# Channel MLP: the second product by seven half-size block products, token-major output

## Chip, cores and metric

One core of one Trainium2 chip. The metric is device time in microseconds (us), median of the runs of one program; lower is better. The program is written in Python for the five engines of the core: TensorE (PE, matmuls), VectorE (DVE), ScalarE (ACT), GpSimd (POOL) and SyncE (SP, here only a DMA queue).

## What is computed

A one-layer trunk over 512 tokens of 1,024 channels. Two gated branches and an output projection end in the residual `x`; then comes the part that the change touches:

```
h2 = RMSNorm(x) * g_ffn
f  = square(relu(h2 @ W_up))          # 512 x 4096
x  = x + f @ W_down                   # 4096 -> 1024
out = RMSNorm(x) * g_final            # 512 x 1024
```

All is float32. Each operand of a product is split exactly into two parts (`hi`, `lo`) of the type fp32r, and a product is three matmuls: hi·hi, hi·lo, lo·hi.

## The kernel before, in words

Channels lie on the 128 partitions and tokens on the free axis (`T` = 512), so a tile is 128x512. Weights come as a stream of units of eight 128x128 blocks (512 KB), in the order of use, each into a buffer `wraw`. `split` (L87) writes `whi` on ACT (a copy that rounds) and `wlo` on DVE (raw minus hi, both read from SBUF). `blocks` (L136) hands out the blocks; at each new unit it issues the splits of this unit and the next two, and the loads of the three behind them. `wraw`, `whi` and `wlo` have three buffers each, so a split can run two units ahead of the matmuls and no further. A column tile (`col_tile`, L154) takes one unit in most stages: 24 matmuls of 512 columns into one PSUM bank, with the weight block as the stationary operand and the activations moving.

The order on each engine is made when the program is built: a list scheduler takes, for each engine, the ready instruction that stands first in the program. `later(n, fn)` and `tick()` put work off by column tiles.

The MLP works in four chunks of 1,024 hidden channels. `up(c)` (L512) makes eight column tiles; per tile DVE takes relu times the row scale out of PSUM (L508), ACT squares it (L509), and `parts` splits it into `f_jh`, `f_jl`. Then come eight column tiles `dn` over the chunk (L526), each added to the residual tile `x2[j]` by DVE (L527). In the last chunk four tiles (`dl`) are done whole, and four (`dh`) by halves of the tokens, with 256 columns per matmul (L595 to L602), so that the final norm of one half can run beside the matmuls of the other. The final norm (`post` L539, `rms_out` L554, `finish` L569) sums squares over the partitions by matmuls with ones, spreads 1/rms by a product with a diagonal, and scales the residual tiles. The output is channel-major and is transposed on the host.

GpSimd does little: sums of squares (L191, L493) and one product per recurrent tile (L421). One pool, `tp`, holds 78 tiles of 128x512 for everything but the weights.

Of the kernel before, what the change touches and what calls it, by code (L numbers as in the profile page):

```python
# [30 lines left out]
# order of the column tiles between the spatial gating's inputs and the output projection  # L31
# [18 lines left out]

@with_exitstack
def trunk(ctx: ExitStack, tc: tile.TileContext, xT, wall, lruw, wsT, par, ln, out):
# [5 lines left out]
    tp = ctx.enter_context(tc.tile_pool(name="tp", bufs=78))  # L58
    ps = ctx.enter_context(tc.tile_pool(name="ps", bufs=8, space=bass.MemoryType.PSUM))

    def t2(name, dt=F32, shape=None):
        return tp.tile(shape or [P, T], dt, tag="t2", name=name)

    def psum(name):
        return ps.tile([P, T], F32, tag="ps", name=name)

# [36 lines left out]
    now = [0]  # L103
    due = {}

# [9 lines left out]
    raws, units = {}, {}  # L115
    n_stream = n_units - KT // 2
    pos = [0]

    def load_unit(u, pieces=1):
        if u < n_stream and u not in raws:  # L120
            raws[u] = wp.tile([P, UB * P], F32, tag="wraw", name=f"wraw{u}")
            n = UB * P // pieces
            for i in range(pieces):
                nc.sync.dma_start(out=raws[u][:, i * n : (i + 1) * n], in_=wall[u][:, i * n : (i + 1) * n])

    def split_unit(u, pieces=1):
        if u < n_stream and u not in units:
            hi = wp.tile([P, UB * P], F32R, tag="whi", name=f"whi{u}")
            lo = wp.tile([P, UB * P], F32R, tag="wlo", name=f"wlo{u}")
            n = UB * P // pieces  # L130
            for i in range(pieces):
                sl = slice(i * n, (i + 1) * n)
                split(raws[u][:, sl], hi[:, sl], lo[:, sl])
            units[u] = (hi, lo)

    def blocks(n=1):  # L136
        u, s = divmod(pos[0], UB)
        if s == 0:
            units.pop(u - 1, None)
            split_unit(u)  # L140
            split_unit(u + 1)
            split_unit(u + 2)
            for i in range(3, 6):
                load_unit(u + i)
        pos[0] += n
        sl = slice(s * P, (s + n) * P)
        return units[u][0][:, sl], units[u][1][:, sl]
# [34 lines left out]
    def x_in(k):  # L182
        xg[k] = parts(f"xg{k}", xts[k], pc(C_GMIX + k))
# [61 lines left out]
    u_t = [[t2(f"u{b}_{h}") for h in range(2)] for b in range(NB)]  # L245
# [46 lines left out]
    # softplus(-lam) = max(-lam, 0) + log1p(exp(-|lam|)), log1p(e) = 2 atanh(e / (2 + e))  # L292
# [26 lines left out]
    # layer norm of v, one group of channels  # L319
# [15 lines left out]
    # mixing over positions, gating by u, back to channels on partitions  # L335
# [56 lines left out]
        # per head, its channels' both parts stacked along the contraction  # L392
# [11 lines left out]
    def lru_gates(j, xr, xs):  # L404
# [12 lines left out]
        # 1 - a^2 = tanh(-log a) (1 + a^2)  # L417
# [61 lines left out]
    x2, x2g = [], []  # L479
    ssq2 = t2("ssq2")  # L480
    for j in range(KT):
        xt = t2(f"xres{j}")
# [3 lines left out]
        x2g.append(parts(f"x2{j}", xt, pc(C_GFFN + j)))  # L486
# [19 lines left out]
    def up_out(f, name, acc):  # L506
        t = t2(name)
        nc.vector.scalar_tensor_tensor(out=t, in0=acc, scalar=0.0, in1=r2_b, op0=ALU.max, op1=ALU.mult)  # L508
        nc.scalar.activation(t, t, AF.Square)  # L509
        f.append(parts(name, t))  # L510

    def up(c):  # L512
        f = []
        for j in range(FT):
            acc = col_tile(f"up{c}_{j}", x2g)
            if c == 0:
                later(1, lambda acc=acc, j=j: up_out(f, f"f{c}_{j}", acc))
# [13 lines left out]
    f = up(NCH - 1)  # L531
    HT = T // 2
    HK = KT // 2
    HB = NB // 2
    r3 = const.tile([P, NB], F32, name="r3")

    ssq3 = t2("ssq3")

    def post(j, acc, b0, b1):  # L539
        sl = slice(b0 * P, b1 * P)  # L540
        nc.vector.tensor_tensor(out=x2[j][:, sl], in0=acc, in1=x2[j][:, sl], op=ALU.add)  # L541
        if j == 0:
            nc.scalar.activation(ssq3, x2[j], AF.Square)
            return
        sq = t2(f"sqc{j}_{b0}")
        nc.scalar.activation(sq[:, sl], x2[j][:, sl], AF.Square)  # L546
        if j < KT - 1:
            nc.vector.tensor_tensor(out=ssq3[:, sl], in0=ssq3[:, sl], in1=sq[:, sl], op=ALU.add)
        return sq

    # 1/rms with tokens on partitions, then spread over the partitions by a product with its diagonal
    dg = {}

    def rms_out(h):  # L554
        b0, b1 = h * HB, (h + 1) * HB
        ms3 = [psum(f"ms3_{b}") for b in range(b0, b1)]
        for i, s in enumerate((ssq3, sq7[h])):
            for b in range(b0, b1):
                nc.tensor.matmul(
                    ms3[b - b0][:, 0:2], s[:, b * P : (b + 1) * P], ones[:, 0:2], start=i == 0, stop=i == 1  # L560
                )
# [33 lines left out]
    for h in range(2):  # L595
        sl = slice(h * HT, (h + 1) * HT)
        for j in range(HK, KT):
# [5 lines left out]
            if h == 1 and j == HK:  # L603
                rms_out(0)
# [78 lines left out]
```

## Time and profile before

| what | us |
|---|---|
| median of 3 runs (lowest, highest) | 815.52 (815.16, 816.07) |
| span of the profiled execution, first to last instruction | 814.2 |
| PE busy, share of the span | 804.2, 99% |
| DVE busy | 450.9, 55% |
| ACT busy | 398.2, 49% |
| POOL busy | 39.8, 5% |

No time beside its span is listed for the profiled execution; the median lies 1.3 us above the span, which is what lies around it. "Busy" is the time in which an engine has an instruction under way. A line such as "L90 DVE TENSOR_TENSOR wlo<-wraw,whi 128x1024" names the line of the kernel, the engine, the operation, what it writes and reads, and its shape; a number in brackets at the end is the idle time before it and what ended it.

### The profile page before, as it was taken

The numbers are of one execution on the slowest core, as the hardware profiler recorded it, in microseconds if no ns is written. First come the engines' busy times: TensorE is split into PE (matmuls) and PEld (weight loads), VectorE is DVE, ScalarE is ACT, GpSimd is POOL, SyncE is SP. The second block draws the span as 40 slices with busy tenths as digits, with TensorE's granted clock in tenths as the row PEclk, the third lists the DMA queues.
The fourth block names the chain that finished last, engine by engine and source line by source line (L and its number), as shares of the span: only waits on it lengthen the run. The fifth ranks groups of instructions, "written<-read, shape, count | busy, mean of one in ns | idle before, by whom it ended". The sixth has DMA issues, their size and how long they took to land.

```text
span 814.2 us, 9244 instructions
## 1 busy us (share of the span) xinstructions
PE 804.2 (99%) x3656; PEld 669.8 (82%) x3656; DVE 450.9 (55%) x627; ACT 398.2 (49%) x505; POOL 39.8 (5%) x44
## 2 busy tenths in 40 slices
PE   9999999999999999999999999999999999999995
PEld 8788888888888888888888888888888888888895
DVE  5868775786566566665544554344333443344435
ACT  6453546868788888852234443124322432233411
POOL 4200000000000000000003100000000000000000
PEclk9999999999999999999999999999999999999997
DMA  7523321223323233333244322322332233223202
GB/s 261 175 98 117 116 91 56 101 69 103 114 77 107 88 104 103 104 104 103 84 137 155 103 92 93 114 88 94 103 104 85 97 104 104 83 98 121 87 1 103
DMA packets 27595, 84.27 MB, mean 103 GB/s; under 512 B 3233, under 2 KB 5281, under 8 KB 27553
## 3 DMA queue, kind: packets, MB, share of 16 engines
q1 hardware_dynamic: 23728, 77.67, 28.6%
q10 hardware_dynamic: 3824, 6.03, 2.4%
q8 instruction: 28, 0.46, 0.2%
q14 instruction: 15, 0.11, 0.0%
HBM read 81.59 MB, written 2.10 MB: 103 GB/s over the span
## 4 chain that ended last, share of the span: by engine, by line
PE 96%; POOL 1%; DMA 1%; SPq 0%; DVE 0%; ACT 0%; issue 0%; DVEq 0%; POOLq 0%
PE up L152 7%; PE up L150 7%; PE up L151 7%; PE dn L152 5%; PE dn L150 5%; PE u L225 5%; PE dn L151 5%; PE v L225 3%; PE g L150 2%; PE x L152 2%; PE x L150 2%; PE g L152 2%; PE ba L152 2%; PE ba L151 2%; PE x L151 2%; PE g L151 2%
## 5 line engine op out<-in xcount | busy, mean ns | idle before, releaser
L89 ACT ACTIVATE whi<-wraw 128x1024 fp32r<-128x1024 f32 (+1 forms) x139 | 145.3, 1051 | 289.8 <-PE dn L151 101.4
L90 DVE TENSOR_TENSOR wlo<-wraw,whi 128x1024 fp32r<-128x1024 f32 (+1 forms) x139 | 170.8, 1229 | 40.0 <-ACT whi L89 39.7
L508 DVE SCALAR_TENSOR_TENSOR f<-up,r_b 128x512 f32<-128x512 f32 x32 | 22.1, 691 | 79.9 <-PE up L152 79.8
L527 DVE TENSOR_TENSOR xres<-dn,xres 128x512 f32<-128x512 f32 x24 | 16.6, 692 | 78.3 <-PE dn L152 78.3
L425 DVE SCALAR_TENSOR_TENSOR w<-w,s 128x512 f32<-128x512 f32 x10 | 6.9, 692 | 59.3 <-ACT w L420 59.3
L389 DVE SCALAR_TENSOR_TENSOR xr<-xrp,par_sb,xr 128x512 f32<-128x512 f32 x30 | 22.5, 750 | 0.7
L395 ACT ACTIVATE xra<-xr 64x512 fp32r<-64x512 f32 x10 | 6.3, 633 | 31.3 <-DVE xr L389 31.3
L421 POOL TENSOR_TENSOR ig<-ig,xr 128x512 f32<-128x512 f32 x10 | 12.9, 1287 | 156.6 <-ACT ig L415 144.8
L509 ACT ACTIVATE f<-f 128x512 f32<-128x512 f32 x32 | 19.8, 619 | 1.4 <-DVE f L508 1.4
L546 ACT ACTIVATE sqc<-xres 128x256 f32<-128x256 f32 (+1 forms) x11 | 5.2, 476 | 29.0 <-DVE xres L541 29.0
L493 POOL TENSOR_TENSOR ssq<-ssq,sqb 128x512 f32<-128x512 f32 x7 | 11.5, 1649 | 100.5 <-issue 79.6
L485 DVE TENSOR_TENSOR xres<-o,xres 128x512 f32<-128x512 f32 x8 | 5.5, 691 | 19.7 <-PE o L152 17.2
L452 ACT ACT_TABLE_LOAD x11 | 14.1, 1283 | 0.2
L415 ACT ACTIVATE ig<-gate,par_sb 64x512 f32<-64x512 f32 x20 | 13.7, 684 | 0.4
L415 ACT ACTIVATE rg<-gate,par_sb 64x512 f32<-64x512 f32 x20 | 13.7, 683 | 0.4
L437 ACT ACT_TABLE_LOAD x10 | 12.8, 1283 | 0.3 <-DVE gr L436 0.2
L426 ACT ACT_TABLE_LOAD x10 | 12.8, 1283 | 0.2
L418 ACT ACT_TABLE_LOAD x10 | 12.8, 1283 | 0.2
L150 PE MATMUL up<-x20h,whi 128*128 128x512 f32 x32 | 12.9, 402 | 0.0
L151 PE MATMUL up<-x27l,whi 128*128 128x512 f32 x32 | 12.5, 390 | 0.0
L150 PE MATMUL up<-x22h,whi 128*128 128x512 f32 x32 | 12.5, 390 | 0.0
L152 PE MATMUL up<-x24h,wlo 128*128 128x512 f32 x32 | 12.5, 390 | 0.0
(953 smaller groups left out, 2372.1 us busy)
## 6 DMA issues: line engine op xcount, KB each, us to landing
wraw<-in_wall SPq DMA_DIRECT2D x137, 512.0 KB, 3.3
xt<-in_xT SPq DMA_DIRECT2D x8, 256.0 KB, 6.2
xres<-in_xT ACTq DMA_DIRECT2D x8, 256.0 KB, 2.6
lr<-in_wall SPq DMA_DIRECT2D x8, 256.0 KB, 5.7
lwr<-in_lruw ACTq DMA_DIRECT2D x5, 256.0 KB, 2.7
ln<-in_ln ACTq DMA_DIRECT2D x4, 256.0 KB, 5.0
out_yT<-o ACTq DMA_DIRECT2D x4, 256.0 KB, 2.3
wraw<-in_wall SPq DMA_DIRECT2D x2, 256.0 KB, 4.1
```

The lines of the kernel that those rows point to most:

```text
L89: nc.scalar.activation(hi, src, AF.Copy)
L90: nc.vector.tensor_tensor(out=lo, in0=src, in1=hi.bitcast(F32), op=ALU.subtract)
L150: nc.tensor.matmul(acc, lhs[0], rhs[0], start=start, stop=False)
L151: nc.tensor.matmul(acc, lhs[0], rhs[1], start=False, stop=False)
L152: nc.tensor.matmul(acc, lhs[1], rhs[0], start=False, stop=stop)
L225: nc.tensor.matmul(acc[b], xg[k][xi][:, b * P : (b + 1) * P], w[wi], start=k == 0 and i == 0, stop=k == KT - 1 and i == 2,)
L389: nc.vector.scalar_tensor_tensor(out=xr, in0=xrp[:, 1 + k : 1 + k + T], scalar=pc(C_CW + k * RT + j), in1=xr, op0=ALU.mult, op1=ALU.add)
L415: nc.scalar.activation(dst[o], acc[n][src], AF.Sigmoid, bias=par_sb[o, c + j : c + j + 1])
L452: nc.scalar.activation(gs, gs, AF.Sigmoid)
L508: nc.vector.scalar_tensor_tensor(out=t, in0=acc, scalar=0.0, in1=r2_b, op0=ALU.max, op1=ALU.mult)
L509: nc.scalar.activation(t, t, AF.Square)
L527: nc.vector.tensor_tensor(out=x2[j], in0=acc, in1=x2[j], op=ALU.add)
```

## The change

Per chunk the second product is a product of A (512 tokens x 1,024 hidden) with B (1,024 hidden x 1,024 channels). Both are cut into 2x2 blocks of 512, and seven products of blocks and of sums of blocks replace the eight (the Winograd form of Strassen's scheme; `PRODUCTS` is their order). Now the activations are the stationary operand and the weights move, so the result has tokens on partitions.

- **Weights**: W_down comes as eight raw tiles of 128x1024 per chunk, loaded during `up(c)`. `sum_item` makes the sums of the weight blocks on GpSimd, in place: two instructions of 128x1024 each for p5, p6, p7, p4. Each of the 14 items (seven products, two halves) is then split like a unit, through the same three buffers.
- **Activations**: `up_out` squares into 128x(4x256) tiles `a11`..`a22`. `factor` makes `s5`, `s6` on DVE and two sums (for p3, p7) on GpSimd, and splits the factor of each product.
- **Matmuls**: per product 2 x 4 x 3 = 24 of 512 columns. Three pairs of PSUM banks (`d`, `e`, `f`) are summed over several products and added to the residual by DVE, 14 adds of 128x512 per chunk, issued with a raised priority.
- **Residual**: eight `turn_x2` in the first `up` transpose it to token-major tiles `xk` (four 128x128 transposes and one ACT copy each).
- **Final norm**: `square` sums squares along the free axis on ACT, `finish` scales by 1/rms per partition and the gains; no matmuls, and the output needs no transposing.
- **Pools**: `tp` has 54 tiles; 24 (`xp`, later `x2p`) hold the scaled input and `u`, later the residual and its parts. `mp` takes the place of `tp` in the MLP.

The core of the diff:

```diff
+PRODUCTS = ("p1", "p2", "p5", "p6", "p3", "p7", "p4")
-    tp = ctx.enter_context(tc.tile_pool(name="tp", bufs=78))
+    xp = x_stack.enter_context(tc.tile_pool(name="xp", bufs=24, side="right", reuse_waits="tile"))
+    tp = t_stack.enter_context(tc.tile_pool(name="tp", bufs=54, reuse_waits="tile"))
...
+    def sum_item(n):
+        if n >= len(items) or items[n][0] != "d" or n in summed:
+            return
+        summed.add(n)
+        _, c, q, h = items[n]
+        terms = {
+            "p5": ("b12", "b12", "b11"), "p6": ("b12", "b22", "b12"), "p7": ("b11", "b12", "b11"), "p4": ("b21", "b21", "b12")
+        }.get(q)
+        if terms:
+            out_, in0, in1 = (dn_raw[c, x, h] for x in terms)
+            nc.gpsimd.tensor_tensor(out=out_, in0=in0, in1=in1, op=ALU.subtract)
...
+    def item():
+        n = pos[0]
+        pos[0] += 1
+        ready.pop(n - 1, None)
+        for i in range(3):
+            split_item(n + i)
+        for i in range(3, 8):
+            if i < 5 or (n + i < len(items) and items[n + i][2:3] in (("p7",), ("p4",))):
+                sum_item(n + i)
+        for i in range(3, 6):
+            load_item(n + i)
+        if items[n][0] == "u" and items[n][1] >= n_first:
+            load_down(*divmod(items[n][1] - n_first, FT))
+        return ready[n]
...
+    def factor(c, a, q):
...
+        for out_, in0, in1, op in {
+            "p5": [("s5", "a21", "a22", ALU.add)],
+            "p6": [("s6", "s5", "a11", ALU.subtract)],
+            "p3": [("a12", "a12", "s6", ALU.subtract)],
+            "p7": [("a11", "a11", "a21", ALU.subtract)],
+        }.get(q, []):
+            eng = nc.vector if q in ("p5", "p6") else nc.gpsimd
+            eng.tensor_tensor(out=a[out_], in0=a[in0], in1=a[in1], op=op)
+        src = a[{"p1": "a11", "p2": "a12", "p5": "s5", "p6": "s6", "p3": "a12", "p7": "a11", "p4": "a22"}[q]]
+        hi, lo = (mp[0].tile([P, HK, HT], F32R, tag=f"f{x}", name=f"f{x}{c}{q}", bufs=3) for x in "hl")
+        split(src, hi, lo)
+        return hi, lo
+
+    def down(c, a, done):
+        fac = {q: factor(c, a, q) for q in PRODUCTS[:2]}
...
+            def mm(j, h):
+                for kk in range(2 * h, 2 * h + 2):
+                    lhs = tuple(x[:, kk, j * P : (j + 1) * P] for x in (fh, fl))
+                    rhs = tuple(x[:, (kk - 2 * h) * T : (kk - 2 * h + 1) * T] for x in w[h])
+                    for i, (li, ri) in enumerate(((0, 0), (0, 1), (1, 0))):
+                        nc.tensor.matmul(
...
+            if q in ("p7", "p4"):
+                w[1] = item()
+                for j in range(2):
+                    for h in range(2):
+                        mm(j, h)
+            else:
+                mm(0, 0)
+                mm(1, 0)
+                w[1] = item()
+                mm(0, 1)
+                mm(1, 1)
...
+            for j in range(2):
+                x = xk[2 * th + j][nh]
+                with tc.high_priority(offset=AHEAD):
+                    nc.vector.tensor_tensor(out=x, in0=bank[k][j], in1=x, op=ALU.add)
...
+    def square(b, h):
+        sq = mp[0].tile([P, T], F32, tag="ft", name=f"sqc{b}_{h}", bufs=3)
+        nc.scalar.activation(sq, xk[b][h], AF.Square, accum_out=s3[:, b, h : h + 1])
+
+    def finish(b):
+        nc.vector.tensor_tensor(out=r3[:, b : b + 1], in0=s3[:, b, 0:1], in1=s3[:, b, 1:2], op=ALU.add)
+        nc.scalar.activation(r3[:, b : b + 1], r3[:, b : b + 1], AF.Sqrt, bias=eps_t, scale=1.0 / D)
+        nc.vector.reciprocal(r3[:, b : b + 1], r3[:, b : b + 1])
+        for h in range(2):
+            o = mp[0].tile([P, T], F32, tag="ft", name=f"o{b}_{h}", bufs=3)
+            nc.vector.scalar_tensor_tensor(
+                out=o, in0=xk[b][h], scalar=r3[:, b : b + 1], in1=gfin[0][:, h * T : (h + 1) * T],
...
```

## Rows read from the trace of the kernel before

**Rows 1.** The page: busy time of each engine, and the chain that ended last

```profile
PE 804.2 (99%) x3656; PEld 669.8 (82%) x3656; DVE 450.9 (55%) x627; ACT 398.2 (49%) x505; POOL 39.8 (5%) x44
...
PE 96%; POOL 1%; DMA 1%; SPq 0%; DVE 0%; ACT 0%; issue 0%; DVEq 0%; POOLq 0%
```

**Rows 2.** Stretches: bounds, length, busy us per engine (instructions), granted clock, DMA share, GB/s

```profile
545.50:589.00 43.50, 43.50 (x193) 36.05 (x192) 20.69 (x24) 17.92 (x24) 0.00 (x0) 1.00 0.29 97
589.00:632.50 43.50, 43.50 (x193) 36.06 (x192) 15.34 (x16) 8.50 (x8) 0.00 (x0) 1.00 0.29 97
```

**Rows 3.** Chain in order of time: the same place of the first and third chunk's dn

```profile
503.94 0.45 PE dn L151 x2
...
678.02 0.45 PE dn L151 x2
```

**Rows 4.** PE in order of time: the last chunk's dl begins, dh begins, dh ends

```profile
757.65 0.39 PE L150 MATMUL dl<-f_0h,whi 128*128 128x512 f32 x1
...
779.41 0.28 PE L150 MATMUL dh<-f_0h,lw_0h 128*128 128x256 f32 x1
...
803.65 0.28 PE L152 MATMUL dh<-f_7h,lw_1l 128*128 128x256 f32 x1
```

**Rows 5.** Waits, in total: who released ACT's weight split

```profile
ACT whi L89 <- PE dn L151: 101.4, 24, 5.7
```

**Rows 6.** DVE in order of time, output projection: one instruction right behind another

```profile
420.58 1.23 DVE L90 TENSOR_TENSOR wlo<-wraw,whi 128x1024 fp32r<-128x1024 f32 x1 [0.83 <-ACT whi L89]
421.72 0.69 DVE L485 TENSOR_TENSOR xres<-o,xres 128x512 f32<-128x512 f32 x1
...
426.36 0.69 DVE L485 TENSOR_TENSOR xres<-o,xres 128x512 f32<-128x512 f32 x1 [2.41 <-DMA xres<-in_xT]
426.97 1.21 DVE L90 TENSOR_TENSOR wlo<-wraw,whi 128x1024 fp32r<-128x1024 f32 x1
```

**Rows 7.** DVE in order of time, first stage, while POOL adds squares

```profile
11.73 0.74 DVE L93 SCALAR_TENSOR_TENSOR xg2l<-xt,par_sb,xg2h 128x512 fp32r<-128x512 f32 x1
...
14.37 1.78 DVE L93 SCALAR_TENSOR_TENSOR xg3l<-xt,par_sb,xg3h 128x512 fp32r<-128x512 f32 x1
...
17.78 1.78 DVE L93 SCALAR_TENSOR_TENSOR xg5l<-xt,par_sb,xg5h 128x512 fp32r<-128x512 f32 x1
19.48 2.31 DVE L90 TENSOR_TENSOR wlo<-wraw,whi 128x1024 fp32r<-128x1024 f32 x1
21.72 1.78 DVE L93 SCALAR_TENSOR_TENSOR xg6l<-xt,par_sb,xg6h 128x512 fp32r<-128x512 f32 x1
23.42 1.78 DVE L93 SCALAR_TENSOR_TENSOR xg7l<-xt,par_sb,xg7h 128x512 fp32r<-128x512 f32 x1
```

**Rows 8.** POOL in order of time: an add alone, and one issued beside DVE

```profile
428.82 1.29 POOL L493 TENSOR_TENSOR ssq<-ssq,sqb 128x512 f32<-128x512 f32 x1 [3.72 <-ACT sqb L492]
432.70 1.79 POOL L493 TENSOR_TENSOR ssq<-ssq,sqb 128x512 f32<-128x512 f32 x1 [2.59 <-ACT sqb L492]
```

**Rows 9.** ACT by shape: the weight split, and a 512 square

```profile
L89 ACT ACTIVATE whi<-wraw 128x1024 fp32r<-128x1024 f32 x137 | 144.1, 1057 | 288.4 <-PE dn L151 101.4 <-PE up L151 93.0 <-issue 47.2
L546 ACT ACTIVATE sqc<-xres 128x512 f32<-128x512 f32 x3 | 1.9, 632 | 8.8 <-DVE xres L541 8.8
```

**Rows 10.** Chain in order of time: transposes of the gating branch

```profile
121.41 0.44 PE ybT L353 x4
```

**Rows 11.** The end, in order of time, all engines

```profile
803.97 0.42 DVE L541 TENSOR_TENSOR xres<-dh,xres 128x256 f32<-128x256 f32 x1 [0.49 <-PE dh L152]
...
805.83 0.17 DVE L564 RECIPROCAL r<-r 128x2 f32<-128x2 f32 x1 [1.44 <-ACT r L563]
...
807.70 3.22 DVE L577 SCALAR_TENSOR_TENSOR o<-xres,par_sb,rb 128x256 f32<-128x256 f32 x8 [1.18 <-PE rb L573]
```

**Rows 12.** Stretches of the end, columns as in Rows 2

```profile
805.00:806.00 1.00, 0.50 (x4) 0.42 (x4) 0.17 (x1) 0.48 (x2) 0.00 (x0) 0.97 0.00 0
806.00:807.00 1.00, 0.53 (x2) 0.56 (x3) 0.48 (x3) 0.00 (x0) 0.00 (x0) 0.50 0.00 0
```

More of the change, by code (lines that the diff above doesn't have):

```diff
@@ L112, in tick @@
             fn()
-    raws, units = {}, {}
-    n_stream = n_units - KT // 2
-    pos = [0]
[L119 to L134, printed above, removed]
@@ L136, in blocks @@
[L136 to L147 removed]
+    n_first = n_units - NCH * FT
+    items = [("u", u) for u in range(n_first)]
+    for c in range(NCH):
+        items += [("u", n_first + c * FT + j) for j in range(FT)]
+        items += [("d", c, q, h) for q in PRODUCTS for h in range(2)]
@@ new lines, in trunk, with load_item, load_down @@
+    raws, ready, summed = {}, {}, set()
+    dn_raw = {}
+    pos = [0]
+    def load_item(n, pieces=1):
+        if n >= len(items) or items[n][0] != "u" or n in raws:
+            return
+        u = items[n][1]
+        raws[n] = wp.tile([P, UB * P], F32, tag="wraw", name=f"wraw{u}")
+        w = UB * P // pieces
+        for i in range(pieces):
+            nc.sync.dma_start(out=raws[n][:, i * w : (i + 1) * w], in_=wall[u][:, i * w : (i + 1) * w])
+    def load_down(c, j):
+        q, h = ("b11", "b21", "b12", "b22")[j // 2], j % 2
+        t = dn_raw[c, q, h] = mp[0].tile([P, 2 * T], F32, tag="raw", name=f"raw{c}{q}{h}", bufs=8)
+        nc.sync.dma_start(out=t, in_=wdn[c, j])
@@ new lines, in sum_item, with split_item @@
+    def sum_item(n):
+        if n >= len(items) or items[n][0] != "d" or n in summed:
+            return
+        summed.add(n)
[6 more added lines that the diff above has]
+            nc.gpsimd.tensor_tensor(out=out_, in0=in0, in1=in1, op=ALU.subtract)
+    def split_item(n, pieces=1):
+        if n >= len(items) or n in ready:
+            return
+        hi = wp.tile([P, UB * P], F32R, tag="whi", name=f"whi{n}")
+        lo = wp.tile([P, UB * P], F32R, tag="wlo", name=f"wlo{n}")
+        if items[n][0] == "u":
+            src = raws.pop(n)
+        else:
+            _, c, q, h = items[n]
+            sum_item(n)
+            src = dn_raw[c, {"p1": "b11", "p2": "b21", "p5": "b12", "p6": "b12", "p3": "b22", "p7": "b11", "p4": "b21"}[q], h]
+        w = UB * P // pieces
+        for i in range(pieces):
+            sl = slice(i * w, (i + 1) * w)
+            split(src[:, sl], hi[:, sl], lo[:, sl])
+        ready[n] = (hi, lo)
@@ L552, in trunk @@
[L552 to L561, printed above, removed]
-        for b in range(b0, b1):
-            nc.scalar.activation(r3[:, b : b + 1], ms3[b - b0][:, 0:1], AF.Sqrt, bias=eps_t)
-        nc.vector.reciprocal(r3[:, b0:b1], r3[:, b0:b1])
-        for b in range(b0, b1):
-            dg[b] = t2(f"dg{b}", F32, [P, P])
-            nc.vector.tensor_scalar(out=dg[b], in0=ident, scalar1=r3[:, b : b + 1], scalar2=None, op0=ALU.mult)
@@ L613, in _blocks @@
+    for c in range(NCH):
+        a = up(c)
+        down(c, a, last if c == NCH - 1 else lambda q: None)
+    assert pos[0] == len(items) and block[0] == UB
 def _blocks(w, cols):
```

183 lines of the change are left out of this document (90 added, 93 removed).

## The prediction, made before the change was run

> **What bounds the kernel now.** I read the page first: PE is busy for 99% of the span, and it is 96% of the chain that ended last [rows 1]. So a matmul taken out is time taken out, as long as PE stays fed. Then the stretches of the MLP. An `up` and a `dn` of one chunk are 43.5 us each, PE never idle, its granted clock 1.00; DVE is busy for 20.7 us of an `up` and for only 15.3 us of a `dn`, ACT for 17.9 and 8.5, POOL for nothing [rows 2]. Two chunks are 174.08 us apart at the same place [rows 3], so one takes 87.04 us; with 384 matmuls of 512 columns that is 0.2267 us per matmul. The last `down` is dearer: from the first `dl` to the end of the last `dh` it is 803.77 - 757.65 = 46.1 us; its 192 half-width matmuls, with the norm's small ones among them, take 24.4 [rows 4], where 96 whole ones would take 21.8. The four downs together are 3 x 43.5 + 46.1 = 176.7 us.
>
> Two views say what feeds PE. ACT's weight split waits for PE's last use of a buffer [rows 5]: the splits run as early as the three buffers allow. And DVE gives up one 128x1024 split every 1.14 us when its queue is full, one 128x512 add out of PSUM every 0.61 us [rows 6].
>
> **The change, part by part.**
>
> *Matmuls.* 7 x 24 = 168 per chunk in place of 192: 168 x 0.2267 = 38.1 us, and 152.3 us for four. On PE alone the downs give back 176.7 - 152.3 = 24.4 us.
>
> *Transposes.* Eight times four, in the first `up`, on PE: 8 x 0.44 [rows 10] = 3.5 us added. Their ACT copies (0.63 us by the nearest row [rows 9]) lie beside the matmuls.
>
> *Tail.* Before, 814.2 - 803.8 = 10.4 us follow the last matmul. After: 0.2 until DVE starts as before, add 0.69 [rows 6], square 0.63 [rows 9], two steps of about 0.2 like the reciprocal and one Sqrt of 0.3, two scalings 1.3, and from the end of the last scaling to the end of the span 814.2 - 810.9 = 3.3 as before [rows 11]: 6.9 with the handovers. Gain 3.5, which pays for the transposes. So the time is 815.5 + (sum of the four downs after - 176.7). The sum is made against the span of 814.2; the 1.3 around it are carried over.
>
> *What feeds the products.* This decides. A product takes PE 5.44 us and asks for two weight splits (before: one per 5.44 us), one split of its factor, and two adds out of PSUM; p5 and p6 also a DVE sum each. POOL makes ten sums of 128x1024 per chunk. Two of them (p5) need only raw weights, so POOL can make them in the `up`. The other eight can't be: p6's overwrites `b12`, which p5's split must have read, and that split waits for a weight buffer; p7's and p4's read p6's result; the two sums of activations need `s6`, hence the last `up` tile.
>
> DVE alone would manage. Between the end of `up` and the last item's split it has 12 weight splits, 6 factor splits and 2 sums, 20 x 1.14 = 22.8 us, and 14 adds x 0.61 = 8.5 us, 31.3 of 38.1. But these 20 have two operands in SBUF, and so have POOL's. In the first stage both engines have such work queued, and there a DVE instruction of 0.74 us takes 1.78, and a split of 1.23 takes 2.31; successive ones start 1.70 us apart [rows 7]: each waits 1.04 to 1.08 us for one 128x512 sum of POOL, in turn. POOL's sum, 1.29 us alone, takes 1.79 beside DVE [rows 8]. They shut each other out. I take 2 x 1.04 = 2.08 us for a 128x1024 sum; no row shows that size. The bounds are 1.04 (if it didn't grow) and 2.57 (twice the whole 1.29). Nearest is the doubled hold, as DVE's own pitch nearly doubles from 512 to 1024.
>
> One down after, from the end of the last `up` tile:
> - 1.3 until the first split is ready for DVE: 0.2 and ACT's 1.06 [rows 9].
> - 22.8 for DVE's 20 two-operand instructions and 8 x 2.08 = 16.6 for POOL's, one after the other.
> - the adds that neither hides. 12 lie before the last split, 12 x 0.61 = 7.3. They read one operand from PSUM; no row shows such an add beside POOL. Bounds: 0 (all run while POOL holds DVE's splits out) and 7.3. POOL holds for 16.6 of some 45 us, so I leave two thirds, 4.6.
> - 4.1 after the last split: p4 needs its second half after 6 of 24 matmuls, 18 x 0.2267 remain.
>
> Sum 49.4, against 38.1 on PE and 43.5 before: PE waits for 11 us in each down, mostly in p6, p3 and p7, the products whose weights or factors need POOL. The next chunk's first split and the last adds fall into the next `up`. Four downs 197.6, **815.5 + 197.6 - 176.7 = 836.4**. Splits can't be pulled ahead: a weight split is at most two items, 5.4 us, before its use. With the ends: adds 0 gives 44.8 per down, 818; adds 7.3 gives 52.1, 847; POOL's sum at 2.57 gives 53.3, 852; at 1.04 it gives 41.1, 803.
>
> The Trainium skill ("SBUF — State Buffer", section "Who interferes with whom") says that a VectorE instruction with at most one SBUF input does not contend with GpSimd. By it the adds would go beside POOL's sums wherever the queue lets them, and the sum would lean to 818; no run here shows it.
>
> *Edits with one answer.* The weights are the same bytes, but come in the `up`: twice the 97 GB/s [rows 2], at a DMA share of 0.29, so 0.6; free. ACT in a down: 14 + 6 splits of 1.06 are 21 us of 49, free; in an `up` two half-width squares replace square and split, less than the 17.9 it had. The adds have priority: while one waits for PE's bank, splits queued behind it wait too; PE's two items ahead cover that, and if they are used up it is part of the 11 us. p7 and p4 follow each other on the same banks, with 2.7 us for each add of 0.7: nothing, unless a split of 1.1 and a POOL hold stand before it, then about 1 us per chunk, within the 7.3. `tp` has 54 tiles where `tp` less the tiles of `xp` had 54 before: nothing to lose but shared spares, bounds 0 and 3 us. Loads into `mp` wait for old tiles of the output projection, all read before the first `up` ends: 0.
>
> **Rivals.**
>
> *POOL's sums don't set the end (faster).* If POOL holds DVE out for less per sum, or its sums meet DVE's idle time, PE stays the bound: downs of 38.1 to 41 us (the 3 for buffers that p7 frees late), **791 to 803, say 797**. For it: DVE alone fits, and DVE's work outside the downs is light. Against it: rows 7 show strict turns. It decides at a down of 44.2: by the list above at 1.43 us per sum in place of 2.08, or at five and a half sums in the down in place of eight.
>
> *PE's clock falls (slower still).* After the dense matmuls end at 803.8 the granted clock is 0.97 in the stretch from 805 and 0.50, the 1.2 GHz level, from 806 [rows 12], with PE busy about half the time. PE's waits in a down may come in pieces of several us. Then a product after such a wait takes up to 10.9 us in place of 5.4; part hides, since DVE is late anyway. One product per down at 3 to 5 us net: 12 to 20 more, **about 850**. Against it: 38 of 49 us stay busy. The Trainium skill ("TensorE: Matmul & The Clock Gate", section "Loop structure matters more than you think") says that a wait for data between bursts of matmuls drops the clock; rows 12 agree on the fall at the end, and no row shows a wait inside dense work.
>
> *A tie.* All adds hidden and POOL's turns packed: 44.5 us per down, about 816 to 818.
>
> **How the numbers follow.** Forecast (818 to 848) 55%, clock 12%, tie 5%, faster 28%. A measurement of this kernel can tell 0.2%, 1.6 us, from no change: faster 0.28, same 0.05, slower 0.67. The range reaches from the middle of the faster case to the upper bound of POOL's sum and into the clock's case: 796 to 853; some 12% lie below and 7% above. Of the forecast alone it would be 818 to 852.
>
> **What would show it.** PE: downs of 168 matmuls in about 49 us, idle before matmuls of p6, p3, p7 ended by DVE's `wlo` or factor splits. DVE: splits of 128x1024 well above 1.23 us in the downs, as in rows 7, and back at 1.23 in the `up`s; a mean near 1.7. POOL: 40 sums of 128x1024, 2.3 us alone and about 3.3 in turns with DVE. Granted clock 1.00 outside the tail. Tail near 7 us. I am wrong if downs take 41 us or less, if the splits keep 1.23 us beside POOL, or if PE's idle time is ended by PSUM adds or DMA.

## The result, and the profile after

The changed kernel takes **866.16 us** (median of 4 runs, 864.65 to 869.72) against 815.40 for the kernel before on the same chip: ratio 1.0626, 95% interval 1.0601 to 1.0651. The direction was right, and the time lies 30 us above the forecast and 13 above the range. The profiled execution is the slowest of the four (869.72 us), with a span of 867.9 us, 53.7 more than the 814.2 of before, where the medians differ by 50.8; the sums below are made in spans.

The page of the changed kernel, busy time, granted clock and the chain that ended last, as in [rows 1]:

```profile
PE 816.6 (94%) x3472; PEld 657.3 (76%) x3472; DVE 568.8 (66%) x656; ACT 436.9 (50%) x565; POOL 165.1 (19%) x83
...
PEclk9999999999999999999999999899989998999988
...
PE 79%; DVE 14%; issue 4%; ACT 1%; POOL 1%; DMA 0%; SPq 0%; DVEq 0%; ACTq 0%; POOLq 0%
```

PE does 184 matmuls fewer, and yet is busy for longer; DVE now has 14% of the chain, where it had none. The stretches of the MLP, columns as in [rows 2]: `up` and `down` of the second chunk (the third's take 44.98 and 53.88 us).

```profile
562.79:607.76 44.97, 44.97 (x193) 36.18 (x192) 17.60 (x18) 14.14 (x24) 0.00 (x0) 1.00 0.23 82
607.76:661.75 53.99, 42.13 (x169) 33.00 (x168) 49.83 (x35) 20.78 (x22) 31.23 (x10) 0.94 0.25 88
```

Two things are to be seen. A `down` takes 54 us, DVE is busy for 50 of them, and POOL makes ten sums in it, not eight. And an `up`, which the change left alone on PE, takes 45.0 us in place of 43.5, with PE never idle and at clock 1.00. The first matmul of successive column tiles of `up`, PE in order of time:

```profile
574.03 0.40 PE L211 MATMUL up<-x20h,whi 128*128 128x512 f32 x1
579.65 0.40 PE L211 MATMUL up<-x20h,whi 128*128 128x512 f32 x1
```

A tile takes 5.62 us, 0.2342 per matmul; it was 5.44 and 0.2267. The same holds in every earlier stage that reads `xg`; the first `up` starts at 459.66, where before it started at 452.10.

The waits of PE in the second chunk's `down`, in order of time; the brackets give the idle time and what ended it:

```profile
621.38 0.50 PE L641 MATMUL f<-wlo,fh1p 128*128 128x512 f32 x1 [2.09 <-DVE wlo L102]
...
625.85 0.50 PE L641 MATMUL f<-wlo,fh1p 128*128 128x512 f32 x1 [1.46 <-DVE wlo L102]
...
632.70 0.80 PE L641 MATMUL d<-wlo,fh1p 128*128 128x512 f32 x1 [3.84 <-DVE wlo L102]
...
634.15 0.63 PE L641 MATMUL d<-wlo,fh1p 128*128 128x512 f32 x1
...
642.65 0.50 PE L641 MATMUL f<-wlo,fh1p 128*128 128x512 f32 x1 [1.69 <-DVE wlo L102]
...
656.15 0.47 PE L641 MATMUL d<-whi,fh1p 128*128 128x512 f32 x1 [2.78 <-DVE xk L661]
```

They are p5 (both halves), p6, p3 and p4; I had named p6, p3 and p7, and p7 waits for nothing. Against the step of 0.2267 these waits are 13.0 us, and the matmuls behind the wait at p6, with 0.63 in place of 0.39, lose 2.6 more: 38.1 + 13.0 + 2.6 = 53.7. What DVE did meanwhile, and POOL (the same stretch, in order of time):

```profile
614.57 0.68 DVE L661 TENSOR_TENSOR xk<-d,xk 128x512 f32<-128x512 f32 x1
615.17 2.83 DVE L102 TENSOR_TENSOR fl1p<-s1p,fh1p 128x1024 fp32r<-128x1024 f32 x1
617.93 0.68 DVE L661 TENSOR_TENSOR xk<-d,xk 128x512 f32<-128x512 f32 x1
618.53 2.79 DVE L102 TENSOR_TENSOR wlo<-raw1b,whi 128x1024 fp32r<-128x1024 f32 x1
621.24 1.21 DVE L102 TENSOR_TENSOR fl1p<-s1p,fh1p 128x1024 fp32r<-128x1024 f32 x1
622.38 3.41 DVE L102 TENSOR_TENSOR wlo<-raw1b,whi 128x1024 fp32r<-128x1024 f32 x1
625.72 1.27 DVE L661 TENSOR_TENSOR xk<-e,xk 128x512 f32<-128x512 f32 x2
626.91 2.44 DVE L102 TENSOR_TENSOR fl1p<-a12f,fh1p 128x1024 fp32r<-128x1024 f32 x1
629.27 3.37 DVE L102 TENSOR_TENSOR wlo<-raw1b,whi 128x1024 fp32r<-128x1024 f32 x1
632.57 1.27 DVE L661 TENSOR_TENSOR xk<-f,xk 128x512 f32<-128x512 f32 x2
```

```profile
613.66 3.26 POOL L616 TENSOR_TENSOR a12f<-a12f,s1p 128x1024 f32<-128x1024 f32 x1 [56.58 <-DVE s1p L616]
616.89 3.35 POOL L616 TENSOR_TENSOR a11f<-a11f,a21f 128x1024 f32<-128x1024 f32 x1
621.40 3.31 POOL L167 TENSOR_TENSOR raw1b<-raw1b,raw1b 128x1024 f32<-128x1024 f32 x1 [1.16 <-DVE wlo L102]
625.87 15.64 POOL L167 TENSOR_TENSOR raw1b<-raw1b,raw1b 128x1024 f32<-128x1024 f32 x5 [1.16 <-DVE wlo L102]
651.95 5.70 POOL L167 TENSOR_TENSOR raw2b<-raw2b,raw2b 128x1024 f32<-128x1024 f32 x2 [10.44 <-DMA raw2b<-in_wdn]
```

The picture of [rows 7] came, at double size: a split beside a POOL sum takes 2.4 to 3.4 us in these rows, and 1.21 in the gap of POOL's row between 620.2 and 621.4, while an add out of PSUM keeps its 0.68 beside POOL. The last row shows the two sums too many: they are the **next** chunk's (`raw2b`), made in p4, because its raw tiles are loaded as soon as the old ones are free.

The sum closes: the four downs are 53.9 + 54.0 + 53.9 + 54.7 = 216.5 us against 176.7, +39.8; the longer step is 7.56 up to the first `up` and 32 x 0.18 = 5.8 in the ups, +13.3; transposes +3.5; the tail, from the last matmul's end (860.4) to the end, is 7.5 in place of 10.4, -2.9. Together 53.7.

### The profile page after: what moved, and what is told of

Same layout as the page of the kernel before. It is cut to its first block, busy times and chain, and to the rows that moved or that the text cites. A ratio compares the mean times of both kernels' runs of the same rounds, so it can differ in the third digit from the quotient of the medians.

```text
span 867.9 us, 9058 instructions
## 1 busy us (share of the span) xinstructions
PE 816.6 (94%) x3472; PEld 657.3 (76%) x3472; DVE 568.8 (66%) x656; ACT 436.9 (50%) x565; POOL 165.1 (19%) x83
## 4 chain that ended last, share of the span: by engine, by line
PE 79%; DVE 14%; issue 4%; ACT 1%; POOL 1%; DMA 0%; SPq 0%; DVEq 0%; ACTq 0%; POOLq 0%
PE up L211 7%; PE up L212 7%; PE up L213 7%; DVE wlo L102 6%; PE v L286 5%; PE u L286 5%; PE d L641 4%; PE g L212 2%; PE x L211 2%; PE g L213 2%; PE x L212 2%; PE g L211 2%; PE x L213 2%; PE ba L211 2%; PE ba L212 2%
## 5 line engine op out<-in xcount | busy, mean ns | idle before, releaser
L101 ACT ACTIVATE whi<-wraw 128x1024 fp32r<-128x1024 f32 (+1 forms) x111 | 116.2, 1049 | 191.9 <-issue 90.9
L102 DVE TENSOR_TENSOR wlo<-wraw,whi 128x1024 fp32r<-128x1024 f32 (+1 forms) x111 | 141.5, 1275 | 45.8 <-ACT whi L101 45.3
L101 ACT ACTIVATE whi<-raw1b 128x1024 fp32r<-128x1024 f32 x14 | 14.8, 1057 | 32.8 <-PE up L212 11.9
L560 POOL TENSOR_TENSOR ssq<-ssq,sqb 128x512 f32<-128x512 f32 x7 | 11.6, 1656 | 101.2 <-ACT sqb L559 101.2
L102 DVE TENSOR_TENSOR wlo<-raw1b,whi 128x1024 fp32r<-128x1024 f32 x14 | 28.1, 2017 | 2.0 <-ACT whi L101 2.0
L102 DVE TENSOR_TENSOR wlo<-raw2b,whi 128x1024 fp32r<-128x1024 f32 x14 | 28.0, 2008 | 2.0 <-ACT whi L101 2.0
L167 POOL TENSOR_TENSOR raw0b<-raw0b,raw0b 128x1024 f32<-128x1024 f32 x8 | 24.7, 3118 | 15.3 <-DMA raw0b<-in_wdn 13.0
L167 POOL TENSOR_TENSOR raw2b<-raw2b,raw2b 128x1024 f32<-128x1024 f32 x8 | 24.7, 3108 | 12.8 <-DMA raw2b<-in_wdn 10.4
L167 POOL TENSOR_TENSOR raw3b<-raw3b,raw3b 128x1024 f32<-128x1024 f32 x8 | 24.6, 3104 | 12.6 <-DMA raw3b<-in_wdn 10.3
L102 DVE TENSOR_TENSOR wlo<-raw0b,whi 128x1024 fp32r<-128x1024 f32 x14 | 25.7, 1854 | 1.4 <-ACT whi L101 1.4
L167 POOL TENSOR_TENSOR raw1b<-raw1b,raw1b 128x1024 f32<-128x1024 f32 x8 | 24.7, 3108 | 10.4 <-DVE wlo L102 10.4
L102 DVE TENSOR_TENSOR wlo<-raw3b,whi 128x1024 fp32r<-128x1024 f32 x14 | 25.9, 1864 | 0.6 <-ACT whi L101 0.6
```

Source lines behind the costliest of these rows:

```text
L101: nc.scalar.activation(hi, src, AF.Copy)
L102: nc.vector.tensor_tensor(out=lo, in0=src, in1=hi.bitcast(F32), op=ALU.subtract)
L167: nc.gpsimd.tensor_tensor(out=out_, in0=in0, in1=in1, op=ALU.subtract)
```

## The experiments

In the tables and texts a **down** is the time between two ups, as above.

### Why do untouched matmuls take longer?

The changed kernel opens its pool `xp` at the right-hand end of SBUF, and in the built program this puts its tiles at byte 180192 and further 2048-byte steps, 32 bytes off a multiple of 64. The other tiles that the matmuls of these stages read, and those of the kernel before, begin at multiples of 64. Two runs moved tiles by 32 bytes, nothing else; the edit of the first (the second has the same pad, without `side`, ahead of `tp` in the kernel before):

```diff
+    pad = ctx.enter_context(tc.tile_pool(name="pad", bufs=1, side="right")).tile([P, 8], F32, name="pad")
+    nc.gpsimd.memset(pad, 0.0)
```

> The changed kernel with the right-hand pool moved down by 32 bytes, so that its tiles begin at multiples of 64 bytes instead of an odd multiple of 32. Theory A (start address): in the changed kernel a column tile over the scaled input or over the residual's parts takes 5.62 us where it took 5.44, 7.6 ns per matmul, because the moving operand begins 32 bytes off; 36 tiles before the output projection and 32 up tiles, 68 x 0.18 = 12.3 us, come back: about 854 us. Rival B (the place at the top of SBUF, or the pool's own bookkeeping, is what slows them): the tiles keep 5.62 us and the time stays at 866.

> The kernel before with the pool of its 78 tiles moved up by 32 bytes, nothing else. Theory A (start address): every column tile pays, some 2,900 matmuls of 512 columns with a moving operand in that pool x 7.6 ns = 22 us: about 838 us, a tile of 24 matmuls at 5.62 us. Rival B (place in SBUF): the place is the same, 815 us.

The kernel before got slower as expected: 836.39 us, ratio 1.0261 (1.0244 to 1.0278). But the changed kernel hardly gained: 864.54 us, ratio 1.0595 (1.0577 to 1.0613), and a tile of `up` still takes 5.60 us. So a start address can cost 20 us, and a multiple of 64 is not what cures it. The tiles that are fast all begin at 320 mod 512; the pad of 32 bytes had made 448. Two more runs: a pad of 160 bytes, which makes 320 (shown against `after_aligned`); and, without a pad, tiles of 2080 bytes, which begin at sixteen different places.

```diff
-    pad = ... .tile([P, 8], F32, name="pad")
+    pad = ... .tile([P, 40], F32, name="pad")
```

> The changed kernel with a pad of 160 bytes ahead of its right-hand pool, so that xg and x2 begin at 64 mod 256 (320 mod 512) like the tiles of the kernel before; the pad of 32 bytes brought 192 mod 256 and hardly helped. Theory A2 (the low bits of the start address beyond the 64-byte step set the price of a moving operand): a column tile of up takes 5.44 us again instead of 5.62, and the time falls by about 72 tiles x 0.18 = 13 us, to 853. Theory B (the right-hand end of SBUF as such, whatever the offset): 5.60 as with the 32-byte pad, 864.

```diff
-        return x2p.tile([P, T], dt, tag="t2x", name=name)
+        return x2p.tile([P, T + 8], dt, tag="t2x", name=name)[:, 0:T]
...
```

> The changed kernel with tiles of 2080 bytes in the right-hand pool, so that the sixteen parts of x2 begin at sixteen different places, 32 to 480 mod 512. Theory A2: the step from a matmul to the next in up differs from part to part, 0.2267 us for the parts at 64 and 320 (the offsets of the kernel before), more for others, and the trace gives the price of each offset. Theory B: all parts cost 0.233 to 0.234.

`pad_160` takes 854.56 us, ratio 1.0473 (1.0454 to 1.0492), 11.6 less than the changed kernel, and its tiles are 5.44 us apart (the granted clock printed for its `up` is 0.95; `early_sums`, with the same pad, has 1.00 and the same 5.44):

```profile
573.33 0.39 PE L213 MATMUL up<-x20h,whi 128*128 128x512 f32 x1
578.77 0.39 PE L213 MATMUL up<-x20h,whi 128*128 128x512 f32 x1
```

`offsets` (863.26 us, one execution) was no help: its tiles take 5.57 us, the steps from a matmul to the next, averaged by part and by half of the weights, lie between 0.227 and 0.236, and the parts at 64 and 320 don't stand out. That already speaks against a price that hangs on one tile's place alone. What is special about 320? The weight tiles begin there too. Three runs of the kernel before part the two:

```diff
+    pad = ctx.enter_context(tc.tile_pool(name="pad", bufs=1)).tile([P, 48], F32, name="pad")
+    nc.gpsimd.memset(pad, 0.0)
     tp = ctx.enter_context(tc.tile_pool(name="tp", bufs=78))
```

> The kernel before with a pad of 192 bytes ahead of its main pool, so that every moving operand begins at 0 mod 512 in place of 320. Theory R (only a start at 320 mod 512, where the weight tiles begin too, gives 0.2267 us per matmul): column tiles of 5.6 us, about 836. Theory Z (a start at a multiple of 256 is as good or better): 5.44 us or less, 815.

`before_all_0` has this pad ahead of the weight pool; `before_weights_0` has it there too, and 320 bytes more ahead of `tp`:

```diff
+    pad = ctx.enter_context(tc.tile_pool(name="pad", bufs=1)).tile([P, 48], F32, name="pad")
...
     wp = ctx.enter_context(tc.tile_pool(name="wp", bufs=3))
+    pad2 = ctx.enter_context(tc.tile_pool(name="pad2", bufs=1)).tile([P, 80], F32, name="pad2")
...
     tp = ctx.enter_context(tc.tile_pool(name="tp", bufs=78))
```

> The kernel before with a pad of 192 bytes ahead of the weight pool, so that weight tiles and all other operands of its matmuls begin at 0 mod 512 together (in the run before_0mod512 the weights stayed at 320). Theory R2 (what counts is that the stationary and the moving operand begin at the same place mod 512): 0.2267 us per matmul again, column tiles of 5.44 us, 815. Theory R (the place 320 mod 512 itself): 5.60 or more, 836 or more.

> The kernel before with the weight tiles at 0 mod 512 and all other tiles at 320 as before. Theory R2: the two operands of a matmul begin at different places, 5.60 us per column tile, 836. Theory M (only the moving operand's place counts, and it must be 320): column tiles of 5.44 us, while v and u, whose moving operand is the weights, take longer.

| run | weights, others (mod 512) | tile of `up`, us | time, us |
|---|---|---|---|
| before | 320, 320 | 5.44 | 815.4 |
| before_all_0 | 0, 0 | 5.44 | 815.59 |
| before_weights_0 | 0, 320 | 5.495 | 823.04 |
| before_0mod512 | 320, 0 | 5.60 | 836.12 |
| before_shifted | 320, 352 | 5.60 | 836.39 |

The three runs with a 0 are single executions; their tiles are alike through all four `up`s. The same row in `before_all_0`, `before_weights_0` and `before_0mod512`:

```profile
550.80 0.39 PE L152 MATMUL up<-x20h,whi 128*128 128x512 f32 x1
556.24 0.39 PE L152 MATMUL up<-x20h,whi 128*128 128x512 f32 x1
```

```profile
550.75 0.39 PE L154 MATMUL up<-x20h,whi 128*128 128x512 f32 x1
556.24 0.39 PE L154 MATMUL up<-x20h,whi 128*128 128x512 f32 x1
561.74 0.39 PE L154 MATMUL up<-x20h,whi 128*128 128x512 f32 x1
```

```profile
575.37 0.39 PE L152 MATMUL up<-x20h,whi 128*128 128x512 f32 x1
580.97 0.39 PE L152 MATMUL up<-x20h,whi 128*128 128x512 f32 x1
```

For whole stages it is neither a right nor a wrong place, but whether the stationary and the moving operand begin at the **same** place: with equal starts 0.2267 us per matmul at 320 and at 0, with unequal ones 0.229 to 0.234. It holds with the roles exchanged: `u`, with `xg` stationary and the weights moving, takes 43.3 us from the start of its first matmul to that of its last in `pad_160`, and 44.6 in the changed kernel. Theory R2's direction held in both last runs; the size did not (823 where it said 836), so the price depends on the difference. It has a sign, too: where the moving operand begins 320 bytes above the stationary one the step is 0.229 in `up` (`before_weights_0`) and in `u` (`before_0mod512`, 43.7 us for 191 steps); where it begins 320 below, 0.233 in both (`up` of `before_0mod512`, `u` of `before_weights_0`, 44.6 us). One thing does not fit: by R2 the part at 320 in `offsets` should have kept 0.2267, and it did not stand out, so what sets the step of a single matmul among unlike neighbours is not shown. Whether 512 is the period, and what on the chip does it, stays open too.

### Whose are the waits in a down?

Three runs took the weight sums from POOL: to DVE (and the two activation sums too), away, or replaced by writes alone.

```diff
-            nc.gpsimd.tensor_tensor(out=out_, in0=in0, in1=in1, op=ALU.subtract)
+            nc.vector.tensor_tensor(out=out_, in0=in0, in1=in1, op=ALU.subtract)
...
-            eng = nc.vector if q in ("p5", "p6") else nc.gpsimd
+            eng = nc.vector
```

> The changed kernel with all ten sums per chunk on DVE instead of POOL. Theory L (DVE and POOL shut each other out while both read two operands from SBUF, so a sum costs the shared port 2.08 us on POOL and 1.14 us on DVE): a down falls from 55.4 us to 1.3 + 28 to 30 two-operand instructions x 1.14 + 12 adds x 0.61, now hidden by nothing, + 4.1 = 45 to 47 us; four downs give back 34 to 42 us: 825 to 832 us. Rival D (DVE is simply overloaded in a down and POOL takes work off it): ten sums more on DVE, 11.4 us per down, 46 us in all: about 910 us.

```diff
-            nc.gpsimd.tensor_tensor(out=out_, in0=in0, in1=in1, op=ALU.subtract)
+            pass
```

> The changed kernel without the eight sums of weight blocks per chunk: the products take the raw blocks, so the sums are left out of the computation. Theory L: without them a down has 20 two-operand instructions of DVE and two sums of POOL, 1.3 + 22.8 + 4.2 + some 5 for adds + 4.1 = 37 us, below PE's 38.1, so downs of 39 to 42 us and 13 to 16 us less each: 802 to 814 us, with PE's clock at full speed in the downs. Rival D (DVE's own queue sets the downs): POOL's work is beside it and the time stays above 855 us. Rival C (the fall of PE's clock makes the time): downs shorten only by what the clock gave away, about 3 us each, 854 us.

```diff
-            nc.gpsimd.tensor_tensor(out=out_, in0=in0, in1=in1, op=ALU.subtract)
+            nc.gpsimd.memset(out_, 0.0)
+            nc.gpsimd.memset(out_, 0.0)
```

> The changed kernel with each of the eight weight sums of a down replaced by two POOL memsets of the tile (the products are not those of the sums). POOL then only writes. Theory L (a two-operand POOL sum and a two-operand DVE instruction go in turns): the splits of DVE beside memsets stay near 1.14 us apart and the time comes near the run without weight sums, 825 to 835. Theory W (it is POOL's own time and the waits for its results that make the downs long, not turns): the waits stay, and the time stays over 850.

| run | time, us | ratio (95%) | downs of the four chunks, us |
|---|---|---|---|
| changed kernel | 866.16 | 1.0626 (1.0601 to 1.0651) | 53.9, 54.0, 53.9, 54.7 |
| sums_on_dve | 852.77 | 1.0457 (1.0441 to 1.0472) | 47.8, 49.4, 50.0, 50.7 |
| weight_memsets | 828.09 | 1.0153 (1.0137 to 1.0170) | 44.5, 43.7, 43.7, 44.6 |
| no_weight_sums | 824.72 | 1.0115 (1.0100 to 1.0130) | 42.0, 43.3, 43.1, 42.6 |

`sums_on_dve` came out between the theory's 825 to 832 and the rival's 910 (the 55.4 us that its text gives for a down are 53.9 to 54.7 in the trace). `no_weight_sums` came out some 10 us above what turns alone had led me to expect, which is the longer step again (all three carry its 13 us); `weight_memsets` came as expected. `weight_memsets` parts POOL's time from its turns. The two sums of activations are still POOL's there, so one trace has both; POOL first, then DVE:

```profile
603.76 3.26 POOL L617 TENSOR_TENSOR a12f<-a12f,s1p 128x1024 f32<-128x1024 f32 x1 [1.52 <-DVE s1p L617]
606.99 3.35 POOL L617 TENSOR_TENSOR a11f<-a11f,a21f 128x1024 f32<-128x1024 f32 x1
...
611.49 0.95 POOL L167 MEMSET raw1b<- 128x1024 f32 x1 [0.25 <-DVE wlo L102]
612.38 1.85 POOL L168 MEMSET raw1b<- 128x1024 f32 x2
```

```profile
605.28 2.83 DVE L102 TENSOR_TENSOR fl1p<-s1p,fh1p 128x1024 fp32r<-128x1024 f32 x1
...
608.63 2.79 DVE L102 TENSOR_TENSOR wlo<-raw1b,whi 128x1024 fp32r<-128x1024 f32 x1
611.35 1.21 DVE L102 TENSOR_TENSOR fl1p<-s1p,fh1p 128x1024 fp32r<-128x1024 f32 x1
612.48 1.21 DVE L102 TENSOR_TENSOR wlo<-raw1b,whi 128x1024 fp32r<-128x1024 f32 x1
```

Beside a sum a split takes 2.8 us, beside a memset 1.21. The downs fall by 10 us, though POOL still has fourteen instructions in one, 17.8 us of busy time. It is the turns. The Trainium skill ("SBUF — State Buffer", section "Who interferes with whom") says that a VectorE instruction with two SBUF inputs contends with a GpSimd instruction that reads SBUF and not with one that only writes it; this trace agrees, with 2.8 and 1.21.

`sums_on_dve` shows that the work itself is too much for a `down`, on either engine: DVE then is busy for 44.3 of 49.4 us, more than PE's 38.1, and PE still waits at p5 and p6, for splits that stand behind the sums.

### Which of the sums set the end, and does the clock?

Two more runs on the changed kernel. The first keeps the next chunk's p5 sums out of p4: its raw loads are held behind the weight loads of `up` on SP's queue.

```diff
-        nc.sync.dma_start(out=t, in_=wdn[c, j])
+        with tc.issue_after(last_load[0].ins):
+            nc.sync.dma_start(out=t, in_=wdn[c, j])
```

> The changed kernel with the loads of the raw down blocks issued on SP only behind the load of the up weights of the same step, so that a chunk's b12 lands some 15 us into its up and its two p5 sums can't be made in p4 of the chunk before. Theory L (each sum of POOL in a down keeps DVE off for about 2.08 us, and two of the ten sums came to the down by the early loads): the first three downs lose two sums each, 3 x 4.2 = 12 us less, 854. Rival F (the first p5 split waits for POOL's queue whenever the sums are made, or the later loads come too late): 864 to 870.

The second gives PE work of no use in its waits, to see what becomes of the clock and of the time.

```diff
+    FILL = {("p5", 0): 8, ("p5", 1): 5, ("p6", 0): 15, ("p3", 0): 6}
...
+                            for i in range(FILL[q, h]):
+                                f = nc.tensor.matmul(fill, x2g[i % KT][0][:, 0:P], x2g[i % KT][0], start=True, stop=True)
```

> The changed kernel with matmuls of no use put on PE where it waits in a down: 8 ahead of p5's first half, 5 ahead of its second, 15 ahead of p6, 6 ahead of p3 (34 x 0.234 = 8.0 us, inside the 9.7 us of these waits in the profile of the changed kernel). Theory C (the matmuls at half clock after the wait at p6, 2.6 us in a down, lie on the path): the granted clock stays at 1.00 through the down, the slow matmuls go, and a down takes 51.3 to 52 in place of 53.9: 856 to 859. Rival H (DVE and POOL are late anyway, so slow matmuls cost nothing): downs of 53.9 and over, 866 or more.

Both theories of mine missed, and the rivals' figures came. `gated_loads` takes 864.71 us (1.0599, 1.0583 to 1.0615) and `pe_filled` 866.17 (1.0607, 1.0589 to 1.0626). Their traces say why. The second chunk's `down` of `gated_loads`, columns as in [rows 2]:

```profile
605.68:657.55 51.87, 41.96 (x169) 32.85 (x168) 46.81 (x35) 20.79 (x22) 25.54 (x8) 0.93 0.03 10
```

POOL now makes eight sums in it, and the down lost only 2.1 us: the wait at p4 went from 2.9 to 0.8 us, and hardly anything else moved. And `pe_filled`, two waits and two stretches:

```profile
628.73 0.50 PE L645 MATMUL d<-wlo,fh1p 128*128 128x512 f32 x1 [0.66 <-DVE wlo L102]
...
638.73 0.51 PE L645 MATMUL f<-wlo,fh1p 128*128 128x512 f32 x1 [2.25 <-DVE wlo L102]
```

```profile
636.00:640.00 4.00, 1.75 (x8) 1.12 (x7) 4.00 (x3) 0.67 (x1) 1.59 (x1) 0.99 0.06 13
640.00:644.00 4.00, 4.00 (x12) 3.12 (x11) 3.28 (x4) 1.06 (x1) 0.00 (x0) 0.59 0.90 327
```

At p6 the wait is filled and the slow matmuls are gone; at p3 the wait has grown to 2.25 us, and the clock falls behind that one instead. In the second chunk, from the end of the last `up` tile to the end of p3's wait it is 34.9 us in the changed kernel, 34.9 in `gated_loads`, 34.9 in `pad_160`, 35.0 in `pe_filled`: **DVE and POOL set that point, whatever PE does before it.** Behind it PE has 71 of its 168 matmuls left, 71 x 0.2267 = 16.1 us, which nothing hides, and the wait at p4. So a down is 34.9 + 16.1 + 2.9 = 53.9; with gated loads 34.9 + 16.1 + 0.8 = 51.8. Slow matmuls ahead of that point are free, and behind it they cost their time: `pe_filled`'s 35.0 + 16.1 + 1.2 = 52.3 became 54.1, and the third down of `gated_loads`, with its clock falling behind p3, took 53.4 where the second took 51.9.

### The sums at another place

In an `up` DVE has 27 us idle. The next kernel makes the weight sums there, on DVE, into tiles of their own; p6 to p4 get six, in the room that the residual's tiles leave after the first `up` and in `mp`. It also splits `a11` and forms `a11 - a21` in `up`, loads the raw tiles in the first four steps, and has the pad of 160 bytes. Its core:

```diff
+            if j == 4:
+                a["p1"] = factor(c, a, "p1")
+                nc.vector.tensor_tensor(out=a["a11"], in0=a["a11"], in1=a["a21"], op=ALU.subtract)
+            q = {3: "p5", 4: "p6", 5: "p7", 6: "p4"}.get(j)
+            if q and (c > 0 or j < 5):
+                with tc.issue_after(up_ins[0].ins):
+                    weight_sum(c, q)
...
-            "p6": [("s6", "s5", "a11", ALU.subtract)],
+            "p6": [("s6", "a22", "a11", ALU.subtract)],
```

> All sums on DVE, the eight weight sums of a chunk made during its up into tiles of their own (the xres tiles are free by then), a11 split and a11-a21 formed in up too, the raw blocks loaded in the first four steps of up, the right-hand pool at 64 mod 256. DVE has left in a down 14 + 6 splits, 3 sums and 14 adds: 23 x 1.14 + 14 x 0.62 = 34.9 us against 38.1 of PE. Theory L with A2 (place of the sums, turns with POOL and the pool's address are the whole loss): a down takes 39 to 41 us, an up 43.5, and the time is 800 to 808, faster than the kernel before at 815.4. Rival (DVE's sum over up and down counts, or the shorter waits come back elsewhere): 820 to 840.

The last one gives those weight sums back to POOL, still in `up`, with the loads held as in `gated_loads` (shown against `early_sums`, without the edit of the loads).

```diff
-            nc.vector.tensor_tensor(out=out_, in0=in0, in1=in1, op=ALU.subtract)
+            nc.gpsimd.tensor_tensor(out=out_, in0=in0, in1=in1, op=ALU.subtract)
```

> As early_sums, but the eight weight sums of a chunk are POOL's, and the raw loads are held behind the up loads so that the sums fall into the up. Theory P (the place decides, not the engine: in an up DVE has 27 us idle, and taking turns costs nothing there): a down as in early_sums, 41 us, and the time within 806 to 812. Rival E (POOL's sums are dear wherever they are, since the splits of up wait behind them and PE's ups grow): over 820.

`early_sums` takes **807.65 us**, ratio 0.9898 (0.9880 to 0.9916): 1.0% less than the kernel before, a small gain with an interval clear of 1, at the upper end of what was expected. `early_sums_pool` takes 812.41, ratio 0.9958 (0.9941 to 0.9975), just above the expected 806 to 812. The second chunk's `up` and `down` of `early_sums`, then of `early_sums_pool`:

```profile
544.38:587.90 43.52, 43.52 (x193) 36.04 (x192) 27.36 (x27) 14.10 (x24) 0.00 (x0) 1.00 0.30 98
587.90:628.65 40.75, 38.67 (x169) 31.38 (x168) 34.27 (x36) 20.82 (x22) 0.00 (x0) 1.00 0.31 103
```

```profile
549.18:592.70 43.52, 43.52 (x193) 36.04 (x192) 26.84 (x19) 13.97 (x23) 22.60 (x8) 1.00 0.50 181
592.70:634.09 41.39, 39.00 (x169) 31.29 (x168) 35.06 (x36) 20.93 (x22) 2.24 (x1) 1.00 0.04 13
```

The `up` did not grow by any of it, and the down is 41 us on either engine, with the clock at 1.00. So the place decides: eight sums of POOL beside DVE are free in an `up`. (The split of `a11` and `a11 - a21` moved into the `up` in both runs; their share of the gain is not parted.) The 5 us between the two kernels are the first chunk's `down` (48.3 against 43.6): there two weight sums of each half can't be made before the residual's tiles are free, and four of POOL's sums fall into that down.

## Why the forecast was right in direction and wrong in size

- **Matmuls, transposes, tail**: right. 168 matmuls per down; a first `up` tile takes 6.06 in place of 5.62, 3.5 us for eight; tail 7.5 where I said 6.9.
- **The turns of DVE and POOL**: right, and the reason why the change is slower. From 608.88 to 643.65 DVE is never idle: 15 two-operand instructions x 1.14 are 17.1 of these 34.8 us, and 17.7 are left for eight sums of POOL and six adds. The rows above part the two. Where no add comes just before, a split beside a sum takes 3.3 us until the next instruction starts (622.38 to 625.72, 629.27 to 632.57), 2.2 more than its 1.14; behind one add it takes 2.76 (615.17 to 617.93), behind two 2.36 (626.91 to 629.27), each add taking about 0.5 to 0.6 off. So a sum keeps DVE's splits off for 2.2 us, close to the 2.08 that I took, and the adds run beside it: 8 x 2.2 is all of the 17.7. Up to here the adds cost next to nothing, where I had let two thirds of their time count; my term for them was too large, the one for the sums slightly too small. POOL's sum takes 3.1 to 3.4 in turns, as I said.
- **The step that failed in the downs** is "4.1 after the last split". I lined up all of DVE's and POOL's work to the last split and let PE finish behind it. POOL is through its eight sums at 641.5, 34 us into the down, and what DVE then has left is lighter than PE's p3, p7 and p4: 16.1 us of matmuls follow the last dear wait, not 4.1. Up to the end of p3's wait, which is the end of DVE's 14th two-operand instruction, my list gives 1.3 + 14 x 1.14 + 8 x 2.08 + 2.3 (half of the 4.6 for adds) = 36.2 where 34.9 were measured; the rest of it is 13.2 where 19.0 were measured, 16.1 of matmuls and the 2.9 of p4's wait. The downs came to 216.5, not 197.6: 18.9 of the miss.
- **"POOL can make [p5's sums] in the `up`"**: wrong. I did not ask when their tiles are loaded. They add 2.1 us at p4, by the one wait that I had put at "about 1 us". That wait is ended by an add out of PSUM, which I had named as a sign of being wrong.
- **The clock** was a rival to my forecast, and came with it. In the second and third down its slow matmuls, 2.6 us in the second, lie ahead of p3's wait and are hidden. In the first and the last down three stretches at 0.50 lie behind it (from 542.6, 556.2 and 853.2, 3.4 us each); eight matmuls of 0.43 in place of 0.23 make about 1.6 us each, 4.8 in all. The rival's 12 to 20 us were not there.
- **"Pools ... bounds 0 and 3 us"** failed: 13.3 us. I had asked what a smaller pool costs, not where the other one begins; [rows 2] and [rows 3] gave 0.2267 per matmul, and I carried it over as a property of PE.
- **The sum of the miss**, in spans: 18.9 + 13.3 + 0.6 for the tail make the 32.8 between the forecast's 20.9 and the measured 53.7.
- **The rival that POOL's sums don't set the end** did not come in the changed kernel; its condition is met in `early_sums`: downs of 41 us, as it said, once the sums are moved.

## To carry to other kernels

Where two engines feed a third through a fixed order of products, find the last wait that they end, and count what the third still has to do behind it; time saved on the third engine ahead of that point gains nothing, and a sum over all the feeding work is not the length. Work that makes two engines take turns belongs into a stage in which one of them is mostly idle, even at the cost of extra tiles. And when a change opens a pool, look at the start addresses: keep the stationary and the moving operands of a stage at the same place mod 512, as the fast runs here have them, or measure what it costs.

## What the runs showed that I had not expected

- A matmul of 512 fp32r columns, with its weight load beside it and no idle gap, takes 0.2267 us when all operands of its stage begin at the same place mod 512, 0.2290 to 0.2342 on average when the two kinds don't. For the kernel before this is worth up to 21 us of 815.
- Adds out of PSUM run beside POOL's two-operand sums at their usual pace, and shorten the time for which the next split is held off (2.76 and 2.36 us in place of 3.3).
- Inside dense work the granted clock fell to 0.50, the 1.2 GHz level, around single waits: in the changed kernel from 631.3 to 638.1, around the 3.84 us at p6, and in `pe_filled` for 3.4 us behind the 2.25 at p3. The length of a wait does not tell it. Here are two waits at p5 in the changed kernel, in its first and its last down, and the stretch around the end of each, columns as in [rows 2]:

```profile
523.31 0.50 PE L641 MATMUL f<-wlo,fh0p 128*128 128x512 f32 x1 [2.79 <-DVE wlo L102]
...
819.19 0.79 PE L641 MATMUL f<-wlo,fh3p 128*128 128x512 f32 x1 [2.09 <-DVE wlo L102]
```

```profile
523.00:527.00 4.00, 3.69 (x16) 3.08 (x17) 4.00 (x5) 0.31 (x1) 3.66 (x2) 1.00 0.00 0
819.00:823.00 4.00, 3.81 (x10) 3.04 (x11) 4.00 (x3) 0.47 (x1) 3.28 (x1) 0.57 0.00 0
```

The longer wait left the clock at 1.00, the shorter one did not; the 2.09 us at p5 in the second down left it at 1.00 too. What decides is not shown here.
